# A decoder layer in fp32 on one core: feature blocks of one size, and six gate pieces released by the first slot matrix

## The chip, the cores and the metric

The kernel runs on 1 core of one Trainium2 chip. The metric is device time in microseconds of the whole program, the median of several runs. All tensors are fp32.

## The reference

One layer on a sequence of 256 tokens of width 2048: a conditioning product gives six vectors (shift, scale and gate for two sub-layers); the first sub-layer is one input projection, sparse attention and a pooling branch, and an output projection; the second is a mixture of 32 experts, of which each token uses two.

```
ada = silu(c) @ w_ada + b_ada
sh1, sc1, gt1, sh2, sc2, gt2 = split(ada, 6)
h = rmsnorm(x, g1) * (1 + sc1) + sh1
q, k, v, qi, ki, wi, p = split(h @ w_in)
mix = concat(dsa_attention(...), multiscale_pool(p)) @ w_out
x = x + gt1 * mix
h2 = rmsnorm(x, g2) * (1 + sc2) + sh2
x = x + gt2 * hier_moe(h2)        # top group, top 2 of its 8 experts, SwiGLU
```

`w_ada` has 2048 x 12288 values (100.7 MB), `w_in` 30.5 MB, `w_out` 16.8 MB, and the expert matrices `w1`, `w3`, `w2` 402.7 MB; all are read once.

## The kernel before

**Conditioning, first two vectors.** `sh1` and `sc1` are needed before the input projection can begin. They are made in blocks of features (`BLOCKS`, L184): two blocks of 256 and three of 512. `block_ada(b)` (L188) loads the columns of `w_ada` that a block needs, in pieces of 1 MB, each by two transfers (L201). For the first two blocks TensorE multiplies the pieces with `silu(c)` into PSUM (L209) and ScalarE evicts the sum (L212); for the others VectorE accumulates them (L217, L219). `block_scales(b)` (L223) sums over the partitions by TensorE (L229) and writes scale and shift (L232 to L234).

**Input projection.** The loop at L539 goes over the blocks: scale and shift of the block, `h` of its features (L543), then the seven `PARTS` of `w_in` with these features as the contraction (`project`, L458). Two of the parts accumulate over all blocks in PSUM (L485); the other results are copied at the first block and added by VectorE at the others (`keep`, L466, L470). `w_in` tiles rotate through four slots (`W_RING`: two halves each of `G2` and `G3`). The pieces of the block after this one are issued between the parts. At the last block the indexer and the pooling sums (L516) run as well.

**The other gates.** `fill_steps` (L320) makes `gt1`, `sc2`, `sh2` and `gt2` in 64 pieces of 1 MB of `w_ada` (16 for each vector) and 4 end steps; `fill(n)` (L337) puts the next n steps at the place at which it is called. A piece is one transfer on SP (L177) and one accumulation by VectorE (L178) into half of `G6`. Its slot comes from a ring of three: `G4` at 0, `G4` at 2048, and `G5`; after the attention the third is `B8` (`LATE_RING`, L113). `FILLS` (L538) names the steps at the parts of the last two blocks, L648 and L699 those during the output projection, and L958 what is left before the experts.

**Output projection, router.** `out_proj` (L602) multiplies the pooling half, then the attention half, with `w_out`, in four parts of 512 columns; VectorE multiplies by the gate and adds (L617, L618). In the attention half `route_block(n)` (L674) follows each part: transposes (L679), copies (L681, L682), router products (L686), squares and `x1c` copies. `route_bias` (L666) multiplies `sh2` with the router's weights (L670) and is called after part 2. Behind it comes the router's chain of small VectorE instructions (L708 to L747), five matmul pairs that count ranks (L741 to L745), and `gather(0)` (L781): the slot matrix `gq` (L786), the combine weights (`weights`, L753), the gather by TensorE (L796) and its eviction to `xg` (L800).

**Experts.** For each quad of four experts `hidden` (L808) loads eight tiles of 2 MB in two halves of the contraction: four of `w1`, four of `w3`, for each half (L815). The tiles go through a ring of seven slots, `G5 G1 G2 G3 G0 G7 G4` (L772), to which `G6` is added after the first quad. So the first half takes `G5 G1 G2 G3` for `w1` and `G0 G7 G4 G5` for `w3`. `down` (L850) loads `w2` in the same way.

**What sets the order.** The program is written in dependency order, and the framework's scheduler (L1000) orders each engine's instructions ahead of the run. An engine executes its instructions in that order, and so does SP with its transfers: a transfer that waits for its slot holds up those behind it.

The lines that the change and the steps below touch: L174 to L180, L184, L195 to L213, L538, L700, L740 to L747, L766 to L768, L787 to L789.

Of the kernel before, what the change touches and what calls it, by code (L numbers as in the profile page):

```python
# [11 lines left out]
AF = mybir.ActivationFunctionType  # L12
ALU = mybir.AluOpType
# [66 lines left out]
def layer_kernel(ctx: ExitStack, tc: tile.TileContext, x, c, w_ada, b_ada, norm1_g, w_in, q_norm_g,  # L80
# [92 lines left out]

    def ada_pieces(sec, acc):  # L174
        def piece(k):
            w = slot([P, D], *fill_ring)
            nc.sync.dma_start(w, w_ada[k * P:(k + 1) * P, sec * D:(sec + 1) * D])  # L177
            nc.vector.scalar_tensor_tensor(acc, w, sT[:, k:k + 1], acc, op0=ALU.mult, op1=ALU.add)  # L178

        return [lambda k=k: piece(k) for k in range(KC)]  # L180
# [3 lines left out]
    BLOCKS = [(0, 2), (2, 2), (4, 4), (8, 4), (12, 4)]  # L184
# [3 lines left out]
    def block_ada(b):  # L188


        k0, nk = BLOCKS[b]
        width = nk * P
        acc = bacc[:, b % 2, :, 0:width]
        per = 1024 // width
        ring = (EARLY_RING, "early") if b < 2 else (BLOCK_RING, "block")  # L195
        held = {}

        def piece(q):
            w = slot([P, per, 2, width], *ring)
            for sec in range(2):  # L200
                nc.sync.dma_start(w[:, :, sec], w_ada2[:, q * per:(q + 1) * per, sec, k0 * P:k0 * P + width])  # L201
            if b < 2:
                if q == 0:
                    held["p"] = bank([P, 2, width], "fl")
                pa = held["p"]
                for kk in range(per):
                    k = q * per + kk
                    g = k % 4
                    nc.tensor.matmul(pa[32 * g:32 * (g + 1)], lhsT=sT[:, k:k + 1].to_broadcast([P, 32]), rhs=w[:, kk],  # L209
                                     start=(k < 4), stop=(k >= KC - 4), skip_group_check=True, tile_position=(0, 32 * g))  # L210
                if q == KC // per - 1:
                    nc.scalar.activation(acc, pa, AF.Copy, scale=1.0 / 32.0)  # L212
                return  # L213
            for kk in range(per):
                k = q * per + kk
                if k == 0:
                    nc.vector.tensor_scalar(acc, w[:, kk], sT[:, 0:1], None, op0=ALU.mult)  # L217
                else:
                    nc.vector.scalar_tensor_tensor(acc, w[:, kk], sT[:, k:k + 1], acc, op0=ALU.mult, op1=ALU.add)  # L219

        return [lambda q=q: piece(q) for q in range(KC // per)]
# [316 lines left out]
    FILLS = {3: (0, 0, 0, 0, 1, 1, 1), 4: (4, 4, 4, 3, 3, 3, 3)}  # L538
# [135 lines left out]
    def route_block(n):  # L674
# [25 lines left out]
        if n == 2:  # L700
            route_bias()
# [38 lines left out]
    pr = bank([P, 3, NE], "sm")  # L740
# [3 lines left out]
    nc.tensor.matmul(pr[:, 2], lhsT=ones, rhs=memf[:, 0], start=True, stop=False)  # L744
    nc.tensor.matmul(pr[:, 2], lhsT=ones, rhs=memf[:, 1], start=False, stop=True)  # L745
    pos = small("pos", NE)
    nc.vector.scalar_tensor_tensor(pos, pr[:, 0:2], 1.0, memf, op0=ALU.add, op1=ALU.mult)  # L747
# [5 lines left out]
    def weights():  # L753
# [12 lines left out]
        nc.vector.scalar_tensor_tensor(over, pr[:, 0:2], float(CAP), cmb, op0=ALU.is_ge, op1=ALU.mult)  # L766
        nc.vector.reduce_max(most, pr[:, 2], axis=AX)
# [13 lines left out]
    def gather(e0):  # L781
# [223 lines left out]
```

## Time and profile before

| | us |
|---|---|
| runs: median (lowest to highest of 3) | 1395.92 (1395.58 to 1398.74) |
| profiled execution: time | 1393.28 |
| profiled execution: span of the instructions | 1391.5 |
| busy: TensorE / VectorE / ScalarE / GpSimd | 1071.9 / 447.1 / 100.0 / 9.1 |
| moved by DMA | 557.27 MB, mean 400 GB/s |

A profile is of one execution. Its span runs from the first to the last instruction; the time of the same execution holds 1.8 us more. Busy time says how long an engine had an instruction at work; whether this work sets the end is read from what waits for it. A row `L613 PE MATMUL mm<-g,mix ... x14` is a group of 14 instructions of line 613 on TensorE that read `g` and `mix` and write `mm`; a matmul of the program appears as two instructions. In brackets stands how long the engine had been idle before it, and what ended that. `PE` is TensorE, `PEld` its weight loads, `DVE` VectorE, `ACT` ScalarE, `POOL` GpSimd, `SP` the engine that issues most transfers.

### The profile page before, as it was taken

To read this page: it belongs to the slowest core of one execution; us is meant where nothing else is said; L and a number is where in the kernel's file an instruction comes from. 1 tells how busy PE (TensorE), PEld (TensorE's weight loads), DVE (VectorE), ACT (ScalarE), POOL (GpSimd) and SP (SyncE) were. 2 spreads that over 40 slices of the span, in tenths; PEclk is the share of its full clock that TensorE was granted. 3 is DMA by queue.
4 is the path that set the end of the run, shared out by engine and by line. 5 is a ranking of instruction groups with operands and counts; after the bars stand their busy time and mean duration, and the time that the engine had idled before them with its cause. 6 is when DMAs were issued, how large, how long until landed. Compare 5 with 4: busy or idle time off the path is not lost.

```text
span 1391.5 us, 12491 instructions
## 1 busy us (share of the span) xinstructions
PE 1071.9 (77%) x5227; PEld 433.6 (31%) x5227; DVE 447.1 (32%) x725; ACT 100.0 (7%) x225; POOL 9.1 (1%) x11
## 2 busy tenths in 40 slices
PE   4899998998997776677758767676776766777566
PEld 2455654544456231122213113121321311222112
DVE  1196667999677210201202111020220202012002
ACT  3200000424222000000000000000000000000000
POOL 1000000000000000000000000000000000000000
PEclk9999999999997979879979988997998998898789
DMA  9999998999999799999999999999999999999997
GB/s 320 328 385 385 400 386 324 342 361 322 400 365 405 325 427 428 427 428 427 427 429 428 428 429 426 427 428 428 428 429 427 428 427 427 428 429 428 429 424 283
DMA packets 101259, 557.27 MB, mean 400 GB/s; under 512 B 18792, under 2 KB 31056, under 8 KB 68688
## 3 DMA queue, kind: packets, MB, share of 16 engines
q1 hardware_dynamic: 97664, 554.22, 97.9%
q10 hardware_dynamic: 3472, 2.20, 0.5%
q8 instruction: 43, 0.70, 0.2%
q14 instruction: 16, 0.13, 0.0%
q0 software_dynamic: 64, 0.02, 0.0%
HBM read 554.31 MB, written 2.10 MB: 400 GB/s over the span
## 4 chain that ended last, share of the span: by engine, by line
DMA 52%; PE 33%; DVE 9%; issue 3%; SPq 2%; ACT 1%; ACTq 0%; DVEq 0%
DMA w<-in_w_dram 49%; PE mm L820 11%; PE mm L475 5%; PE mm L613 5%; PE b L861 4%; PE b L485 3%; DVE g L178 3%; DMA g<-in_w_in_dram 2%; DMA g<-in_w_ada_dram 1%; PE b L877 1%; DVE bacc L219 1%; SPq L815 1%; PE b L796 1%; DVE g L408 1%; DMA v8T<-in_b_ada_dram 1%
## 5 line engine op out<-in xcount | busy, mean ns | idle before, releaser
L820 PE MATMUL mm<-w,xg 128*32 128x512 f32 x2048 | 341.9, 704 | 162.8 <-DMA w<-in_w_dram 162.8
L861 PE MATMUL b<-w,t 128*32 128x512 f32 x896 | 178.0, 671 | 86.5 <-DMA w<-in_w_dram 81.0
L820 PEld LDWEIGHTS mm<-w,xg 128*32 128x32 f32 x2048 | 76.9, 126 | 415.1 <-DMA w<-in_w_dram 229.0
L800 DVE TENSOR_SCALAR xg<-b,sc2T,sh2T 128x128 f32<-128x128 f32 x128 | 42.3, 404 | 390.8 <-PE b L796 390.8
L475 PE MATMUL mm<-g,hT 128*128 128x512 f32 (+1 forms) x320 | 127.6, 553 | 12.0 <-DMA g<-in_w_in_dram 7.1
L178 DVE SCALAR_TENSOR_TENSOR g<-g,sT,g 128x2048 f32<-128x2048 f32 x52 | 122.0, 2346 | 12.2 <-DMA g<-in_w_ada_dram 12.1
L613 PE MATMUL mm<-g,mix 128*128 128x512 f32 x256 | 114.8, 601 | 4.2 <-DVE t L617 4.2
L861 PEld LDWEIGHTS b<-w,t 128*32 128x32 f32 x896 | 41.9, 116 | 217.6 <-DMA w<-in_w_dram 120.5
L841 DVE TENSOR_TENSOR t<-b,gt 128x512 f32<-128x512 f32 (+1 forms) x33 | 20.9, 671 | 273.0 <-PE b L861 250.7
L475 PEld LDWEIGHTS mm<-g,hT 128*128 128x128 f32 x320 | 57.2, 199 | 78.3 <-issue 64.2
L613 PEld LDWEIGHTS mm<-g,mix 128*128 128x128 f32 x256 | 48.2, 193 | 60.7 <-issue 55.1
L844 PE MATMUL mm<-t,gwT 128*128 128x512 f32 (+1 forms) x132 | 62.6, 605 | 3.3 <-DVE t L841 2.8
L796 PEld LDWEIGHTS b<-gq,x1c 128*128 128x128 f32 x512 | 59.8, 196 | 13.1 <-issue 6.7
L796 PE MATMUL b<-gq,x1c 128*128 128x128 f32 x512 | 62.7, 282 | 1.2 <-DVE gq L786 1.2
L824 ACT ACTIVATE t<-mm 128x512 f32<-128x512 f32 x8 | 4.8, 597 | 816.7 <-PE mm L820 816.7
L485 PE MATMUL b<-hT,g 128*128 128x256 f32 x256 | 56.9, 380 | 0.5 <-DMA g<-in_w_in_dram 0.4
L485 PEld LDWEIGHTS b<-hT,g 128*128 128x128 f32 x256 | 48.4, 190 | 11.2 <-issue 3.2
L846 DVE TENSOR_TENSOR xs<-xs,mm 128x512 f32<-128x512 f32 (+1 forms) x66 | 44.3, 671 | 17.7 <-PE mm L844 17.5
L825 DVE TENSOR_TENSOR t<-t,mm 128x512 f32<-128x512 f32 x8 | 5.5, 688 | 116.3 <-PE mm L820 116.3
L219 DVE SCALAR_TENSOR_TENSOR bacc<-g,sT,bacc 128x1024 f32<-128x1024 f32 x28 | 35.9, 1283 | 7.1 <-DMA g<-in_w_ada_dram 4.6
L844 PEld LDWEIGHTS mm<-t,gwT 128*128 128x128 f32 x132 | 21.2, 188 | 45.2 <-DVE xs L846 28.4
L178 DVE SCALAR_TENSOR_TENSOR g<-w,sT,g 128x2048 f32<-128x2048 f32 x12 | 28.1, 2346 | 2.3 <-DMA w<-in_w_ada_dram 2.2
(208 smaller groups left out, 514.4 us busy)
## 6 DMA issues: line engine op xcount, KB each, us to landing
w<-in_w_dram SPq DMA_DIRECT2D x190, 2048.0 KB, 21.3
g<-in_w_ada_dram SPq DMA_DIRECT2D x52, 1024.0 KB, 8.3
g<-in_w_ada_dram SPq DMA_DIRECT2D x44, 512.0 KB, 9.5
g<-in_w_in_dram SPq DMA_DIRECT2D x21, 1024.0 KB, 10.9
g<-in_w_out_dram SPq DMA_DIRECT2D x16, 1024.0 KB, 9.5
w<-in_w_ada_dram SPq DMA_DIRECT2D x12, 1024.0 KB, 7.4
w<-in_w_ada_dram SPq DMA_DIRECT2D x20, 512.0 KB, 9.7
g<-in_w_in_dram SPq DMA_DIRECT2D x14, 512.0 KB, 8.7
```

Of the source, the lines that this page charges most:

```text
L178: nc.vector.scalar_tensor_tensor(acc, w, sT[:, k:k + 1], acc, op0=ALU.mult, op1=ALU.add)
L219: nc.vector.scalar_tensor_tensor(acc, w[:, kk], sT[:, k:k + 1], acc, op0=ALU.mult, op1=ALU.add)
L475: nc.tensor.matmul(po[:, :width], lhsT=hcols(k0 + j, slice(i * P, (i + 1) * P)), rhs=w[:, j], start=(j == 0), stop=(j == nk - 1))
L485: nc.tensor.matmul(ppool[n][:, u], lhsT=w[:, j, u * P:(u + 1) * P], rhs=hcols(k, slice(0, S)), start=(k == 0 and u % 2 == 0), stop=(k == K ...
L613: nc.tensor.matmul(po, lhsT=mix[:, k, i * P:(i + 1) * P], rhs=ws[k // 4][:, k % 4], start=(k == 0), stop=(k == 7))
L796: nc.tensor.matmul(px[:, u], lhsT=x1c[i][:, k // RB, k % RB], rhs=gq[:, i].rearrange("p e s -> p (e s)"), start=(i == 0), stop=(i == NT - 1))
L800: nc.vector.tensor_scalar(xg[:, k], px[:, u], sc2T[:, k:k + 1], sh2T[:, k:k + 1], op0=ALU.mult, op1=ALU.add)
L820: nc.tensor.matmul(h[e * CAP:(e + 1) * CAP, :], lhsT=xg[:, k, e * CAP:(e + 1) * CAP], rhs=ws[e][:, r], start=(k == 0), stop=(k == KC - 1), ...
L841: nc.vector.tensor_mul(y[:, 0:m], py, gt2[:, c0:c0 + m])
L844: nc.tensor.matmul(pz[:, 0:m], lhsT=gwT[:, i], rhs=y[:, 0:m], start=True, stop=True)
L846: nc.vector.tensor_add(xv, xv, pz[:, 0:m])
L861: nc.tensor.matmul(py[n // 2][e * CAP:(e + 1) * CAP, (n % 2) * 512:(n % 2 + 1) * 512], lhsT=aT[:, f, e * CAP:(e + 1) * CAP], rhs=ws[e][:, ...
```

## The change

The first two parts belong to the front of the program. `BLOCKS` has four blocks of 512 features. Only the first is multiplied by TensorE, into two banks instead of one, and its pieces hold 2 rows of 512 values per section where they held 4 of 256; its `w_in` tiles hold four contraction rows instead of two. `FILLS` names the same steps at the last two blocks.

`route_bias` is called one part earlier. The rank counts keep three of five matmul pairs; the two for the maximum go into a bank of their own, inside `weights()`. `weights()` and the product of the combine weights move behind the gather. `gather(0)` puts one column of its slot matrix into `behind`; a piece of `w_ada` that is emitted after that first gets this column copied into its slot by VectorE, and its transfer is issued on GpSimd's queue instead of SP's. These are the last six pieces of `gt2`. The copy is overwritten by the transfer.

```diff
+    behind = []
+
     def ada_pieces(sec, acc):
         def piece(k):
             w = slot([P, D], *fill_ring)
-            nc.sync.dma_start(w, w_ada[k * P:(k + 1) * P, sec * D:(sec + 1) * D])
+            if not behind:
+                nc.sync.dma_start(w, w_ada[k * P:(k + 1) * P, sec * D:(sec + 1) * D])
+            else:
+                nc.vector.tensor_copy(w[:, 0:1], behind[0])
+                nc.gpsimd.dma_start(w, w_ada[k * P:(k + 1) * P, sec * D:(sec + 1) * D])
             nc.vector.scalar_tensor_tensor(acc, w, sT[:, k:k + 1], acc, op0=ALU.mult, op1=ALU.add)
...
-    BLOCKS = [(0, 2), (2, 2), (4, 4), (8, 4), (12, 4)]
+    BLOCKS = [(0, 4), (4, 4), (8, 4), (12, 4)]
...
-        ring = (EARLY_RING, "early") if b < 2 else (BLOCK_RING, "block")
+        ring = (EARLY_RING, "early") if b == 0 else (BLOCK_RING, "block")
...
-                    held["p"] = bank([P, 2, width], "fl")
-                pa = held["p"]
+                    held["p"] = [bank([P, width], "mm") for _ in range(2)]
...
-    FILLS = {3: (0, 0, 0, 0, 1, 1, 1), 4: (4, 4, 4, 3, 3, 3, 3)}
+    FILLS = {2: (0, 0, 0, 0, 1, 1, 1), 3: (4, 4, 4, 3, 3, 3, 3)}
...
-        if n == 2:
+        if n == 1:
             route_bias()
...
-    nc.tensor.matmul(pr[:, 2], lhsT=ones, rhs=memf[:, 0], start=True, stop=False)
-    nc.tensor.matmul(pr[:, 2], lhsT=ones, rhs=memf[:, 1], start=False, stop=True)
...
-        nc.vector.reduce_max(most, pr[:, 2], axis=AX)
+        pm = bank([P, NE], "fl")
+        nc.tensor.matmul(pm, lhsT=ones, rhs=memf[:, 0], start=True, stop=False)
+        nc.tensor.matmul(pm, lhsT=ones, rhs=memf[:, 1], start=False, stop=True)
+        nc.vector.reduce_max(most, pm, axis=AX)
...
         if e0 == 0:
-            weights()
-        nc.vector.tensor_mul(gw, gw, bc(cmb[:, :, e0:e0 + QE, None], QE, CAP))
+            behind.append(gq[:, 1, 0, 0:1])
...
+        if e0 == 0:
+            weights()
+        nc.vector.tensor_mul(gw, gw, bc(cmb[:, :, e0:e0 + QE, None], QE, CAP))
```

**Where instructions move: SP at the start.** Here `g_70`, `g_71`, `g_72` are `G4`, `G5`, `G6`, and `g_68`, `g_69` the slots of `w_in`. Before, behind the transfer of `x`:

```order
L148 DMA xs<-in_x_dram 128x2048 x2
L201 DMA g_70<-in_w_ada_dram 128x4x256 x4
L201 DMA g_71<-in_w_ada_dram 128x4x256 x2
L201 DMA g_72<-in_w_ada_dram 128x4x256 x4
L463 DMA g_68<-in_w_in_dram 128x2x512
L201 DMA w<-in_w_ada_dram 128x4x256 x2
L463 DMA g_68<-in_w_in_dram 128x2x512
L463 DMA g_69<-in_w_in_dram 128x2x512 x2
L625 DMA wr<-in_w_exp_dram 128x8x32
L201 DMA g_70<-in_w_ada_dram 128x4x256 x2
```
After:

```order
L148 DMA xs<-in_x_dram 128x2048 x2
L208 DMA g_70<-in_w_ada_dram 128x2x512 x4
L208 DMA g_71<-in_w_ada_dram 128x2x512 x2
L208 DMA g_72<-in_w_ada_dram 128x2x512 x4
L208 DMA w<-in_w_ada_dram 128x2x512 x2
L471 DMA g_68<-in_w_in_dram 128x4x512 x2
L208 DMA g_70<-in_w_ada_dram 128x2x512
L471 DMA g_69<-in_w_in_dram 128x4x512 x2
L633 DMA wr<-in_w_exp_dram 128x8x32
L208 DMA g_70<-in_w_ada_dram 128x2x512 x3
```
Before, the first eight transfers of `w_ada` are the first block, and the `w_in` tiles come behind them. Now the first block is 16 transfers: the twelve ahead of the first `w_in` tile, and four among the tiles and the router's weights.

**VectorE at the first slot matrix.** Before, from the slots' comparison on (`w` and `g4` are the slots of the pieces, `g6` the accumulator of `gt2`):

```order
L784 TENSOR_TENSOR t2_1899<-kc_76,pos_1892 128x256
L768 CAST mosti_1897<-most_1896 128x1
L786 TENSOR_SCALAR gq_1898<-t2_1899,rs2_1857 128x128 x2
L789 TENSOR_TENSOR t2_1899<-t2_1899,cmb_1894 128x256
L178 SCALAR_TENSOR_TENSOR g6_72<-w_1983,sT_102,g6_72 128x2048
L178 SCALAR_TENSOR_TENSOR g6_72<-g4_70,sT_102,g6_72 128x2048
L800 TENSOR_SCALAR xg_1920<-b2_1921,sc2T_1478,sh2T_1651 128x128 x8
L800 TENSOR_SCALAR xg_1920<-b2_1946,sc2T_1478,sh2T_1651 128x128 x8
L805 COPY gwT_1974<-sm_1971 128x256
L178 SCALAR_TENSOR_TENSOR g6_72<-g4_70,sT_102,g6_72 128x2048
```
After, from the second line behind the slot matrix on (the maximum, L776, stands between):

```order
L811 TENSOR_TENSOR t2_1863<-t2_1863,cmb_1858 128x256
L183 COPY w_1943<-gq_1862 128x1
L777 CAST mosti_1861<-most_1860 128x1
L183 COPY g4_70<-gq_1862 128x1 x2
L808 TENSOR_SCALAR xg_1867<-b2_1868,sc2T_1444,sh2T_1617 128x128 x8
L808 TENSOR_SCALAR xg_1867<-b2_1893,sc2T_1444,sh2T_1617 128x128 x8
L816 COPY gwT_1941<-sm_1938 128x256
L185 SCALAR_TENSOR_TENSOR g6_72<-w_1943,sT_102,g6_72 128x2048
L185 SCALAR_TENSOR_TENSOR g6_72<-g4_70,sT_102,g6_72 128x2048
L183 COPY w_1953<-gq_1862 128x1
L185 SCALAR_TENSOR_TENSOR g6_72<-g4_70,sT_102,g6_72 128x2048
L183 COPY g4_70<-gq_1862 128x1 x2
```
Two of the last three accumulations stood ahead of the evictions to `xg`; now all six stand behind them, and the copies that release the second three pieces stand among these accumulations.

**SP at the first expert loads.** With each tile's number: before, `w_2034`, `w_2036`, `w_2038` are the second to fourth tile of `w3` of the first half (in `G7`, `G4`, `G5`), `w_2072` to `w_2078` those of `w1` of the second half:

```order
L815 DMA w_2034<-in_w3_dram 128x4096
L177 DMA g4_70<-in_w_ada_dram 128x2048
L971 TENSOR_LOAD mosti_1897
L971 ISA x2
L815 DMA w_2036<-in_w3_dram 128x4096
L815 DMA w_2038<-in_w3_dram 128x4096
L815 DMA w_2072<-in_w1_dram 128x4096
L815 DMA w_2074<-in_w1_dram 128x4096
L815 DMA w_2076<-in_w1_dram 128x4096
L856 DMA w_2285<-in_w2_dram 128x4096
```
After, `w_2007`, `w_2009`, `w_2011` are the same three of `w3` (in `G7`, `G4`, `G5`), and `w_2045` to `w_2051` those of `w1`:

```order
L826 DMA w_2007<-in_w3_dram 128x4096
L982 TENSOR_LOAD mosti_1861
L982 ISA x2
L826 DMA w_2011<-in_w3_dram 128x4096
L826 DMA w_2045<-in_w1_dram 128x4096
L826 DMA w_2047<-in_w1_dram 128x4096
L826 DMA w_2049<-in_w1_dram 128x4096
L826 DMA w_2009<-in_w3_dram 128x4096
L826 DMA w_2051<-in_w1_dram 128x4096
L826 DMA w_2085<-in_w3_dram 128x4096
L826 DMA w_2087<-in_w3_dram 128x4096
```
The tile in `G4` stood ahead of the three for the second half; now it stands behind them and behind the tile in `G5`. TensorE uses the four tiles of a half in turn for each contraction row.

## Rows read from the trace of the kernel before

**Rows 1.** The page's slices of 34.8 us each: mean rate of transfers.
```profile
GB/s 320 328 385 385 400 386 324 342 361 322 400 365 405 325 427 428 427 428 427 427 429 428 428 429 426 427 428 428 428 429 427 428 427 427 428 429 428 429 424 283
```

**Rows 2.** Windows: us; busy PE, PEld, DVE, ACT, POOL; PE clock; DMA share; GB/s.
```profile
0.00:12.50 12.50, 0.00 (x0) 0.00 (x0) 0.39 (x2) 0.76 (x1) 0.20 (x4) 1.00 0.86 279
...
12.50:25.00 12.50, 7.50 (x32) 3.53 (x33) 3.59 (x9) 6.19 (x9) 0.00 (x0) 1.00 1.12 337
...
56.00:130.00 74.00, 69.83 (x256) 41.89 (x256) 54.39 (x60) 8.12 (x16) 0.00 (x0) 0.98 1.05 385
...
220.00:240.00 20.00, 16.39 (x55) 7.44 (x54) 20.00 (x34) 0.17 (x1) 0.00 (x0) 0.91 0.89 323
...
320.00:340.00 20.00, 13.36 (x55) 7.93 (x54) 19.89 (x30) 7.44 (x27) 2.29 (x2) 0.91 0.91 315
...
336.00:422.50 86.50, 85.27 (x260) 42.46 (x261) 67.71 (x59) 27.25 (x59) 0.00 (x0) 0.98 0.95 353
...
445.50:460.00 14.50, 14.44 (x118) 10.66 (x122) 13.35 (x24) 0.00 (x0) 0.00 (x0) 0.89 0.52 216
...
460.00:465.00 5.00, 4.33 (x27) 1.14 (x16) 1.01 (x4) 0.59 (x1) 0.00 (x0) 1.00 0.88 308
```

**Rows 3.** TensorE in order of time, to 345 us: start, duration, engine, line, operation.
```profile
30.42 1.05 PE L229 MATMUL sm<-ones,bacc 128*128 128x1 f32 x8 [0.72 <-ACT bacc L212]
...
32.55 3.72 PE L485 MATMUL b<-hT,g 128*128 128x256 f32 x16
...
56.07 13.18 PE L475 MATMUL mm<-g,hT 128*128 128x80 f32 x32 [4.68 <-DMA g<-in_w_in_dram]
...
97.53 7.07 PE L485 MATMUL b<-hT,g 128*128 128x256 f32 x32
...
202.30 13.98 PE L485 MATMUL b<-hT,g 128*128 128x256 f32 x64
```

**Rows 4.** Groups of VectorE's instructions, 216 to 345 us: busy, mean ns | idle before.
```profile
L178 DVE SCALAR_TENSOR_TENSOR g<-g,sT,g 128x2048 f32<-128x2048 f32 x23 | 54.0, 2346 | 0.0
...
L575 DVE SCALAR_TENSOR_TENSOR g<-b,g 128x1024 f32<-128x1024 f32 x2 | 2.4, 1219 | 0.0
...
L578 DVE TENSOR_REDUCE mx<-g 128x4 f32<-128x1024 f32 x2 | 2.4, 1197 | 0.0
```

**Rows 5.** TensorE in order of time, 395 to 500 us.
```profile
411.13 1.42 PE L686 MATMUL sm<-ws,g 128*128 128x36 f32 x12
...
432.64 3.60 PE L686 MATMUL sm<-ws,g 128*128 128x36 f32 x16 [0.39 <-DVE brt L672]
...
443.31 0.61 PE L744 MATMUL sm<-mem,ones 128*128 128x32 f32 x2
...
445.56 8.94 PE L796 MATMUL b<-gq,x1c 128*128 128x128 f32 x64 [1.20 <-DVE gq L786]
...
454.64 7.94 PE L820 MATMUL mm<-w,xg 128*32 128x512 f32 x68
...
472.65 8.76 PE L820 MATMUL mm<-w,xg 128*32 128x512 f32 x60 [2.63 <-DMA w<-in_w_dram]
```

**Rows 6.** VectorE in order of time, 395 to 480 us.
```profile
423.19 2.34 DVE L178 SCALAR_TENSOR_TENSOR g<-w,sT,g 128x2048 f32<-128x2048 f32 x1
...
428.46 0.69 DVE L682 COPY g<-b 128x512 f32<-128x512 f32 x1 [1.11 <-ACT g L681]
...
438.66 2.33 DVE L178 SCALAR_TENSOR_TENSOR g<-g,sT,g 128x2048 f32<-128x2048 f32 x1
...
457.42 2.35 DVE L178 SCALAR_TENSOR_TENSOR g<-g,sT,g 128x2048 f32<-128x2048 f32 x1
```

**Rows 7.** DMA issues: count, KB each, median us to landing.
```profile
g<-in_b_ada_dram POOLq DMA_DIRECT2D x2, 8.0 KB, 5.4
```

**Rows 8.** SP's issues in order of time, 458 to 486 us.
```profile
459.79 4.89 SPq L815 DMA_DIRECT2D w<-in_w_dram  x5
...
480.58 1.75 SPq L815 DMA_DIRECT2D w<-in_w_dram  x4
```

More of the change, by code (lines that the diff above doesn't have):

```diff
@@ L201, in piece @@
                 nc.sync.dma_start(w[:, :, sec], w_ada2[:, q * per:(q + 1) * per, sec, k0 * P:k0 * P + width])
-            if b < 2:
+            if b == 0:
                 if q == 0:
-                    held["p"] = bank([P, 2, width], "fl")
-                pa = held["p"]
+                    held["p"] = [bank([P, width], "mm") for _ in range(2)]
                 for kk in range(per):
@@ L208, in piece @@
                     g = k % 4
-                    nc.tensor.matmul(pa[32 * g:32 * (g + 1)], lhsT=sT[:, k:k + 1].to_broadcast([P, 32]), rhs=w[:, kk],
-                                     start=(k < 4), stop=(k >= KC - 4), skip_group_check=True, tile_position=(0, 32 * g))
+                    for sec, pa in enumerate(held["p"]):
+                        nc.tensor.matmul(pa[32 * g:32 * (g + 1)], lhsT=sT[:, k:k + 1].to_broadcast([P, 32]), rhs=w[:, kk, sec],
+                                         start=(k < 4), stop=(k >= KC - 4), skip_group_check=True, tile_position=(0, 32 * g))
                 if q == KC // per - 1:
-                    nc.scalar.activation(acc, pa, AF.Copy, scale=1.0 / 32.0)
+                    for sec, pa in enumerate(held["p"]):
+                        nc.scalar.activation(acc[:, sec], pa, AF.Copy, scale=1.0 / 32.0)
                 return
@@ L737, in layer_kernel @@
     nc.vector.tensor_scalar(memf, lz, THRESH, None, op0=ALU.is_lt)
-    pr = bank([P, 3, NE], "sm")
+    pr = bank([P, NT, NE], "sm")
     nc.tensor.matmul(pr[:, 0], lhsT=tri, rhs=memf[:, 0], start=True, stop=True)
@@ L743, in layer_kernel @@
     nc.tensor.matmul(pr[:, 1], lhsT=tri, rhs=memf[:, 1], start=False, stop=True)
-    nc.tensor.matmul(pr[:, 2], lhsT=ones, rhs=memf[:, 0], start=True, stop=False)
-    nc.tensor.matmul(pr[:, 2], lhsT=ones, rhs=memf[:, 1], start=False, stop=True)
     pos = small("pos", NE)
-    nc.vector.scalar_tensor_tensor(pos, pr[:, 0:2], 1.0, memf, op0=ALU.add, op1=ALU.mult)
+    nc.vector.scalar_tensor_tensor(pos, pr, 1.0, memf, op0=ALU.add, op1=ALU.mult)
     cmb, over = small("cmb", NE), small("over", NE)
@@ L765, in weights @@
         nc.vector.tensor_mul(cmb, cmb, bc(sg, NE))
-        nc.vector.scalar_tensor_tensor(over, pr[:, 0:2], float(CAP), cmb, op0=ALU.is_ge, op1=ALU.mult)
-        nc.vector.reduce_max(most, pr[:, 2], axis=AX)
+        nc.vector.scalar_tensor_tensor(over, pr, float(CAP), cmb, op0=ALU.is_ge, op1=ALU.mult)
+        pm = bank([P, NE], "fl")
+        nc.tensor.matmul(pm, lhsT=ones, rhs=memf[:, 0], start=True, stop=False)
+        nc.tensor.matmul(pm, lhsT=ones, rhs=memf[:, 1], start=False, stop=True)
+        nc.vector.reduce_max(most, pm, axis=AX)
         nc.vector.tensor_copy(mosti, most)
```

## The prediction

> **What bounds the kernel now.** The page's slices come first: from about 490 us on, the kernel moves 424 to 429 GB/s in every slice but the last, so that part is bound by transfers; before it the rate is between 320 and 405 [rows 1]. The number of bytes does not change. So the end moves by what happens to the moment at which the expert loads begin to run without a break, by what is still unloaded then, and by any break after it.
>
> The windows show what holds the front [rows 2]. Over 0 to 12.5 us 279 GB/s arrive, at 12.5 to 25 us, with `w_ada` in rows of 256 values, 337, and from 56 to 130 us, with rows of 512 values throughout, 385 at a full queue. From 220 to 240 and 320 to 340 us VectorE is busy for 20.00 and 19.89 of 20 us while TensorE stands for 3.6 and 6.6 us: VectorE is the bound there. From 336 to 422.5 us TensorE is busy for 85.27 of 86.5 us: the output projections bound that stretch. From 445.5 to 460 us only 216 GB/s are moved, because no slot is free. TensorE's order in time [rows 3] shows the projections start at 32.55 us, wait 4.68 us until 56.07, and then go on, with the third block (the first of 512 features) at 97.53 and the last block at 202.30 us.
>
> **The first block.** The changed kernel loads 16 half-megabyte transfers of `w_ada` for its first block, where the old one needed 8, and two pairs of `w_in` stand among them in SP's order. Up to the last of the 16, SP has issued `x` 2.1 MB, constants 0.2, `w_ada` 8.4, four `w_in` 4.2 and one router transfer 0.1, or 15.0 MB. By 12.5 us 279 GB/s make 3.5 MB; the other 11.5 MB at 385 GB/s take 29.9 us, so 42.4 us, and I add 1 us for the router transfer's short rows. The matmuls of the last half and the step to the projections follow: the old kernel needed 2.85 us from its last accumulation (the eviction that ends at 30.42 follows one that began at 29.70) to 32.55; eight more column sums take 1.05 us [rows 3]. That gives a start at about 48 us instead of 32.55. The old third and fourth blocks took (202.30 - 97.53) / 2 = 52.4 us each with their waits; the new first block has the same size, so the second starts at 100.4 us, where the old kernel had the same state at 97.53: **+2.9 us**. The early start of the old kernel is worth little because it pays the wait until 56.07 and eight products for the second block in between. Loading 8.4 MB in the longer rows saves 24.9 - 21.8 = 3.1 us of transfers, but the projections, not the transfers, pace the blocks; it is covered, and already in the 385 used above. The block fewer of partial sums (11 additions) falls where VectorE has free time, and costs and gains nothing while the projections go on.
>
> **The middle.** Between the pooling sums and the product of the last pool projection, VectorE's order now holds 26 accumulations of gate pieces where it held 28 (one was moved ahead, one behind), and the last head group's logits and their maximum come after it. At 2.346, 1.219 and 1.197 us [rows 4] this is 4.7 + 2.4 = **-7.1 us**. The work is not gone: it lies beside TensorE's full stretch, where VectorE has 18.8 us free. Bounds of this and the first term together: +5.9 (nothing saved here, and `w_in` comes 3 us late at the second block) and -7.3 us (all 10.2 us of TensorE's idle time in the two windows vanish). I take the sum, -4.2.
>
> **From the output projection to the slot matrices.** `route_bias` moves into TensorE's full stretch. It has 32 instructions; in the full stretch, instructions of the same shape take 1.42 / 12 = 0.118 us [rows 5], so **+3.8 us** (bounds 0, if a hole takes it, and 7.2, at the pace of the 16 at 432.64). In the chain behind, these disappear: the accumulation of 2.34 us between the product and the sum of the last part; the wait for `brt` from the ready copy (428.46 + 0.69) to 432.64, 3.5 us; the accumulation of 2.33 us at 438.66 [rows 6]; two of five matmul pairs of the ranks, from 443.31 on, 0.9 us [rows 5]. Together **-9.0 us**. With `weights()` behind the gather, only `over` stays ahead of the slot matrix, so 0.2 us more is left out.
>
> **The six pieces.** The slot matrix releases them, through one-column copies. Three slots exist, so three pieces can go at once, on POOL's queue. Nothing deep ran on that queue before: an 8 KB transfer took 5.4 us to land on it [rows 7]. At 428 GB/s three pieces (3.15 MB) take 7.35 us, so from the slot matrix (I call the start of its gather g, the old 445.56) they land by about g + 14, in the old gap. Their accumulations stand behind both groups of evictions in VectorE's order, at g + 12 to g + 19, and only they free the slots for the other three. Now the resumption: the first 64 expert instructions ended at 454.64 + 7.5 = 462.1, g + 16.5 [rows 5]; the old SP went on at 459.79, g + 14.2, when the last accumulation at 457.42 [rows 6] freed `G4`, and issued five expert loads [rows 8]. The new SP goes on at g + 16.5, **+2.3 us**, and the three other pieces (3.15 MB) are still to be loaded: **+7.35 us**, as they share the running transfers.
>
> **The slot G4.** Both halves of `G4` hold late pieces, so the third load of the first `w3` half, which needs `G4`, now stands behind four later loads, and SP issues it when the last piece is accumulated, near g + 38. All transfers in flight then end with it: 8.4 + 3.15 + 2.1 MB from g + 18, about g + 50. Every other ring slot is full or in use, and TensorE needs this tile before it can free one. It works through 60 instructions, which took from 472.65 [rows 5] to SP's next issue at 480.58 [rows 8], 7.9 us; the old kernel had further loads queued beside that. Add the landing's signal and the next start: the 308 GB/s of 460 to 465 us [rows 2] are 3.6 us of flow, so the first bytes came at 461.4, 1.6 us after the issue; two loads (4.2 MB) from there should be in at 471.2, and TensorE began at 472.65, 1.4 us later. A new break of **+10.9 us** (bounds 7.9 without these signals, and 16 if POOL's pieces come last).
>
> **Sum.** +2.9 - 7.1 + 3.8 - 9.0 + 2.3 + 7.35 + 10.9 = +11.15 us, about +11. The profiled execution took 1393.28 us around a span of 1391.5, and goes to 1404.4; the median of the runs stands 2.6 us above it, so 1407.
>
> A rule beside the late pieces: on the Trainium skill's page "DMA: Bandwidth & Descriptors" (Queues, rings and completion order) each DMA engine takes turns between the queues that have work, packet by packet. By that rule the three late pieces would not wait for SP's four loads, and the time would be that of the sum and not that of the second rival. No row here shows two deep queues at once.
>
> **The rivals.** (1) My forecast, slower by about 11 us: chance 0.60.
> (2) POOL's pieces are served behind SP's four loads. These 8.4 MB end at g + 38, the pieces at g + 45.6, and the accumulations and the issue of `G4` come some 5 us after the last transfer: +16 us, 1412. For it: the 5.4 us of the only POOL row. Decided by the landing time of the last three pieces. 0.16.
> (3) All six pieces fit into the gap, since the releases come faster than I read them; then the 7.35 us go and +3.8 us is left, 1400, no change that can be told (about 0.3%, 4.2 us, is what a measurement of this kernel tells from none). Against it: the accumulations' place in VectorE's order. 0.12.
> (4) Faster: the output projections are paced by transfers, not by TensorE. Then six pieces less shorten 336 to 422.5 us by 6.3 MB / 428 GB/s = 14.7 us and hide `route_bias`: 11.15 - 14.7 - 3.8 = -7.4, 1388.6. For it: the DMA share of 0.95 in that window [rows 2]. Against it: TensorE idles only 1.2 us there. It decides from the point where a projection waits for `w_out` at all. 0.12. The Trainium skill's page "Trainium Kernel Development and Optimization" (Performance Expectations) calls matmul busy time a bad metric, since matmuls are pipelined. By that rule 85.27 us of busy time would not exclude this rival; the rows at hand agree so far as their instructions of one shape differ in time by the place at which they stand (0.118 and 0.225 us).
>
> **The numbers.** The likeliest gives 1407. Low end: the first terms at -7.3 (3.1 lower) and the break at 7.9 (3.0 lower), one late piece in the gap (2.45): 1398. High end: the second rival, with the first terms near their upper bound: 1417. Slower is 0.60 + 0.16 = 0.76, the same 0.12, faster 0.12.
>
> **What would show it.** Projections that start near 48 us; the second block near 100; no accumulation of gate pieces between the last output projection and the slot matrix, and some 14 us between these two; six `w_ada` transfers on POOL's queue, the first three in the gap, the others beside expert loads; then a slice some 30 us later in which the rate falls, with TensorE at 60 expert instructions and SP waiting for it. The prediction is wrong if no such break is there, if the steady rate begins earlier than before with all of `w_ada` loaded, or if the output projections end much earlier than 422 us.

## The result, and the profile after

The changed kernel takes 1415.16 us in the median of 4 runs (1413.23 to 1417.21), the kernel before 1395.75 beside it: a ratio of 1.0134, 95% interval 1.0118 to 1.0150, so 1.2 to 1.5% slower. Forecast were 1407 and a range of 1398 to 1417. The profiled execution took 1415.19 us around a span of 1413.4, 21.9 more than the span before. The sign and the places were right; the forecast size was little more than half of what came.

The page's slices, as [rows 1] of before:

```profile
GB/s 347 288 382 384 400 376 324 356 384 316 366 316 327 366 291 428 428 428 427 428 427 428 427 429 426 429 426 428 428 428 425 429 429 427 426 429 428 428 425 283
```
The slice from 494.7 to 530.0 us (the fifteenth) has 291 GB/s, between slices of 366 and 428: the new break is there. From then on the rate is what it was.

TensorE in order of time in the front, as [rows 3]:

```profile
42.80 4.92 PE L216 MATMUL mm<-g,sT 128*32 128x512 f32 x12 [5.74 <-DMA g<-in_w_ada_dram]
48.43 1.95 PE L237 MATMUL sm<-ones,bacc 128*128 128x1 f32 x16 [0.70 <-ACT bacc L220]
51.46 5.12 PE L493 MATMUL b<-hT,g 128*128 128x256 f32 x16 [1.08 <-ACT hT L551]
...
99.28 2.83 PE L493 MATMUL b<-hT,g 128*128 128x256 f32 x12
101.95 3.60 PE L483 MATMUL mm<-g,hT 128*128 128x512 f32 x8
...
207.59 13.98 PE L493 MATMUL b<-hT,g 128*128 128x256 f32 x64
...
336.65 13.04 PE L621 MATMUL mm<-g,mix 128*128 128x512 f32 x30
```
and of the kernel before, at the output projection:

```profile
336.43 9.10 PE L613 MATMUL mm<-g,mix 128*128 128x512 f32 x17 [3.45 <-DVE t L617]
```
The input projections start at 51.46 us (forecast 48). At 99.28 the second block has begun, but eight matmul instructions of the first (3.60 us) still stand behind it, so it is really at 102.9, where the old kernel was at 97.53. The last block starts at 207.59 instead of 202.30, 5.3 us late. The first output projection behind VectorE's full stretch starts at 336.65, where the old one started at 336.43 (its wait of 3.45 us ended there): there the changed kernel is only 0.2 us late.

VectorE from the first pooling sum to the first product of the last pool projection, of the kernel before:

```profile
217.36 2.28 DVE L516 TENSOR_TENSOR wa<-g 128x2040 f32<-128x2040 f32 x1 [9.52 <-ACT g L488]
...
348.24 0.68 DVE L617 TENSOR_TENSOR t<-mm,gt 128x512 f32<-128x512 f32 x1
```
and of the changed kernel:

```profile
222.65 2.28 DVE L524 TENSOR_TENSOR wa<-g 128x2040 f32<-128x2040 f32 x1 [9.52 <-ACT g L496]
...
346.13 0.68 DVE L625 TENSOR_TENSOR t<-mm,gt 128x512 f32<-128x512 f32 x1
```
130.9 us have become 123.5. The accumulations of gate pieces in this stretch are 26 where they were 28, and one logits instruction of 1.22 us and one maximum of 1.20 us of the last head group now come behind it.

TensorE from the router's bias on, as [rows 5]:

```profile
418.18 3.66 PE L678 MATMUL sm<-wr,sh2T 128*128 128x36 f32 x32
...
421.85 7.03 PE L621 MATMUL mm<-g,mix 128*128 128x512 f32 x16
...
439.88 0.61 PE L749 MATMUL sm<-mem,kc 128*128 128x32 f32 x2 [3.68 <-DVE mem L745]
...
442.44 9.51 PE L804 MATMUL b<-gq,x1c 128*128 128x128 f32 x64 [0.25 <-DVE gq L795]
...
452.10 7.92 PE L831 MATMUL mm<-w,xg 128*32 128x512 f32 x68
475.42 1.89 PE L831 MATMUL mm<-w,xg 128*32 128x512 f32 x2 [15.41 <-DMA w<-in_w_dram]
482.75 1.91 PE L831 MATMUL mm<-w,xg 128*32 128x512 f32 x2 [5.45 <-DMA w<-in_w_dram]
489.07 1.92 PE L831 MATMUL mm<-w,xg 128*32 128x512 f32 x2 [4.40 <-DMA w<-in_w_dram]
490.92 2.08 PE L298 MATMUL fl<-g,ones 128*128 128x512 f32 x2
...
496.41 2.07 PE L298 MATMUL fl<-g,ones 128*128 128x512 f32 x2 [0.67 <-ACT gt L299]
498.42 8.56 PE L831 MATMUL mm<-w,xg 128*32 128x512 f32 x60
```
and the last output projection of the kernel before:

```profile
416.37 6.17 PE L613 MATMUL mm<-g,mix 128*128 128x512 f32 x14
```
The last output projection ends at 421.85 + 7.03 = 428.88 us, 6.3 after the old one, and the gather starts at 442.44, 13.6 us behind it, where the old kernel needed 23.0. Behind the first 68 instructions (64 of them of `w1`) TensorE stands for 15.4 us, then does one matmul at a time as loads land, then three column sums of `gt2` (L298), and only at 498.42 the 60 instructions of `w3` that free the slots.

VectorE at the last three pieces, as [rows 6]:

```profile
461.91 0.27 DVE L183 COPY g<-gq 128x1 f32<-128x1 f32 x2
472.64 2.35 DVE L185 SCALAR_TENSOR_TENSOR g<-w,sT,g 128x2048 f32<-128x2048 f32 x1 [10.46 <-DMA w<-in_w_ada_dram]
480.09 2.35 DVE L185 SCALAR_TENSOR_TENSOR g<-g,sT,g 128x2048 f32<-128x2048 f32 x1 [5.09 <-DMA g<-in_w_ada_dram]
487.46 2.35 DVE L185 SCALAR_TENSOR_TENSOR g<-g,sT,g 128x2048 f32<-128x2048 f32 x1 [5.02 <-DMA g<-in_w_ada_dram]
```
Two of them were released at 461.91 (the first at 459.53), and they land one in 7.4 us. GpSimd's issues of late pieces have a median of 10.4 and 14.9 us to landing, where the 8 KB of [rows 7] had 5.4.

Windows of 2.5 us (columns as in [rows 2]):

```profile
455.00:457.50 2.50, 2.50 (x28) 0.78 (x24) 2.46 (x2) 0.00 (x0) 0.00 (x0) 1.00 0.03 13
...
460.00:462.50 2.50, 0.01 (x2) 0.00 (x0) 2.18 (x3) 0.00 (x0) 0.64 (x2) 1.00 0.98 295
...
485.00:487.50 2.50, 0.00 (x0) 0.00 (x0) 0.04 (x1) 0.00 (x0) 0.00 (x0) 0.50 1.01 429
487.50:490.00 2.50, 0.93 (x2) 0.18 (x2) 2.50 (x2) 0.00 (x0) 0.00 (x0) 0.50 0.10 39
490.00:492.50 2.50, 2.50 (x4) 0.50 (x2) 1.06 (x4) 0.00 (x0) 0.00 (x0) 0.50 0.69 184
...
495.00:497.50 2.50, 1.83 (x3) 0.50 (x2) 0.00 (x0) 0.59 (x1) 0.00 (x0) 0.50 0.54 229
497.50:500.00 2.50, 2.50 (x10) 0.40 (x12) 0.00 (x0) 0.59 (x1) 0.00 (x0) 0.50 0.04 7
...
505.00:507.50 2.50, 2.50 (x18) 0.64 (x10) 0.00 (x0) 0.00 (x0) 0.00 (x0) 1.00 0.32 66
507.50:510.00 2.50, 0.54 (x2) 0.00 (x0) 0.00 (x0) 0.59 (x1) 0.00 (x0) 1.00 0.81 315
```
The loads go on at 460.8 us and stop at 487.7, 2.1 MB (the tile in `G4`) pass from 491.4 to 496.3, and the flow begins again at 507.8 (counted at 428 GB/s; the first bytes come near 507, at a lower rate). TensorE's clock stands at 0.50, the lower of its levels (1.2 of 2.4 GHz), from 487.5 to 500 us; it had been idle from 460.0 to 475.4.

**One account for every run.** Take the moment at which the expert loads begin to run without a break (the start of the 5 us window plus what it misses to 428 GB/s), the 7.35 us of late pieces still to come at that moment, and the later breaks (what the windows miss to 428 GB/s, summed). What is left of the span is the same in all kernels:

| kernel | loads run from | pieces | breaks | rest | span |
|---|---|---|---|---|---|
| before | 461.4 | 0 | 0 | 930.1 | 1391.5 |
| before, second profile | 466.7 | 0 | 0 | 930.4 | 1397.1 |
| changed | 460.8 | 7.35 | 15.1 | 930.2 | 1413.4 |
| blocks alone | 466.1 | 0 | 0 | 930.5 | 1396.6 |
| no late pieces | 466.8 | 0 | 0 | 931.2 | 1398.0 |
| three late pieces | 461.1 | 0 | 6.4 | 930.3 | 1397.8 |
| two queues | 461.0 | 7.35 | 15.6 | 929.7 | 1413.6 |
| six pieces, `w3` in pairs | 462.3 | 7.35 | 14.4 | 930.2 | 1414.2 |
| two queues, no sums | 461.3 | 7.35 | 6.2 | 930.5 | 1405.4 |
| three pieces, `w3` in pairs | 464.0 | 0 | 0.6 | 930.6 | 1395.2 |
| the same, five blocks | 462.1 | 0 | 0 | 929.9 | 1392.0 |
| router's edits alone | 462.7 | 0 | 0 | 930.2 | 1392.9 |

The pieces and the breaks are 22.45 us; against them the loads resume 0.6 us earlier than in the first profile of before, where the terms of the forecast gave 7.1. The medians lie 19.4 apart and the profiles 21.9, since the first profile of before is 2.5 us below the median beside it. Against the second profile of before the loads resume 5.9 us earlier.

### The profile page after: what moved, and what is told of

The parts are those of the page before. It is cut to its first block, busy times and chain, and to the rows that moved or that the text cites. A ratio compares the mean times of both kernels' runs of the same rounds, so it can differ in the third digit from the quotient of the medians.

```text
span 1413.4 us, 12461 instructions
## 1 busy us (share of the span) xinstructions
PE 1078.0 (76%) x5227; PEld 433.0 (31%) x5227; DVE 443.1 (31%) x717; ACT 99.4 (7%) x225; POOL 12.3 (1%) x17
## 4 chain that ended last, share of the span: by engine, by line
DMA 56%; PE 32%; DVE 6%; SPq 2%; issue 2%; ACT 1%; ACTq 0%; DVEq 0%
DMA w<-in_w_dram 49%; PE mm L831 10%; PE mm L483 5%; DMA g<-in_w_ada_dram 4%; PE b L872 4%; PE mm L621 3%; PE b L493 3%; DVE g L185 2%; DMA g<-in_w_in_dram 2%; PE b L888 1%; SPq L826 1%; DVE g L416 1%; DMA v8T<-in_b_ada_dram 1%; PE fl L298 1%; PE b L804 1%
## 5 line engine op out<-in xcount | busy, mean ns | idle before, releaser
L872 PE MATMUL b<-w,t 128*32 128x512 f32 x896 | 183.2, 690 | 82.8 <-DMA w<-in_w_dram 77.4
L483 PE MATMUL mm<-g,hT 128*128 128x512 f32 (+1 forms) x320 | 123.6, 539 | 3.5 <-DMA g<-in_w_in_dram 1.9
## 6 DMA issues: line engine op xcount, KB each, us to landing
g<-in_w_ada_dram POOLq DMA_DIRECT2D x4, 1024.0 KB, 14.9
```

The lines of the kernel that those rows point to most:

```text
L483: nc.tensor.matmul(po[:, :width], lhsT=hcols(k0 + j, slice(i * P, (i + 1) * P)), rhs=w[:, j], start=(j == 0), stop=(j == nk - 1))
L872: nc.tensor.matmul(py[n // 2][e * CAP:(e + 1) * CAP, (n % 2) * 512:(n % 2 + 1) * 512], lhsT=aT[:, f, e * CAP:(e + 1) * CAP], rhs=ws[e][:, ...
```

## The experiments

Each edit is against the changed kernel where nothing else is said.

**The blocks alone** (the kernel before with the four blocks).

```diff
-    BLOCKS = [(0, 2), (2, 2), (4, 4), (8, 4), (12, 4)]
+    BLOCKS = [(0, 4), (4, 4), (8, 4), (12, 4)]
...
-    FILLS = {3: (0, 0, 0, 0, 1, 1, 1), 4: (4, 4, 4, 3, 3, 3, 3)}
+    FILLS = {2: (0, 0, 0, 0, 1, 1, 1), 3: (4, 4, 4, 3, 3, 3, 3)}
```

> The kernel before with the four blocks of 512 alone. Theory A (the late pieces and the tile in G4 make the loss, the blocks a small part): in the changed kernel the last block began 5.3 us late (207.59 instead of 202.30) and some 2 us of that came back at VectorE's waits, so 3 us slower, 1397 to 1400. Theory B (the blocks make the loss, since the front keeps TensorE waiting longer and all that follows moves with it): 10 us or more, 1406 or later. Theory C (the expert part is paced by transfers, and what the front loses is taken back at the gap of the slots): no change, 1394 to 1397.

1398.36 us (1394.96 to 1400.56), ratio 1.0014 (1.0002 to 1.0027): some 2 us, as theory A has it. TensorE in order of time:

```profile
207.87 13.98 PE L486 MATMUL b<-hT,g 128*128 128x256 f32 x64
...
449.32 9.60 PE L797 MATMUL b<-gq,x1c 128*128 128x128 f32 x64 [1.20 <-DVE gq L787]
```
The last block is as late as in the changed kernel, so that delay belongs to the blocks. So does what comes back of it: the first output projection behind VectorE's full stretch starts at 336.93 us here.

**No late pieces.**

```diff
-        if e0 == 0:
-            behind.append(gq[:, 1, 0, 0:1])
```

> The changed kernel without the late pieces: nothing is put into the list that holds them back, so all of w_ada goes through SP as before; the blocks, the router's bias one part earlier and the weights behind the gather stay. Theory A: the 7.35 us of the three pieces still to be loaded and the break at G4 (15.1 us by the sum of what the windows from 487.5 to 512.5 us miss to 428 GB/s) go, and some of it is given back by accumulations that return to VectorE ahead of the slot matrix: 1392 to 1398, no change to slightly faster than before. Theory B: it keeps most of the loss, 1405 or later.

1398.20 us (1396.04 to 1399.72), ratio 1.0009 (0.9999 to 1.0019), 0.2 us above what theory A gave. No break is left: from 470 to 700 us every window of 5 us has 419 GB/s or more. The late pieces make the loss.

**Three late pieces.**

```diff
         if n < 2:
             fill(9)
+        if n == 2:
+            fill(3)
```

> The changed kernel with three late pieces instead of six: three more steps of the gate pieces are emitted at part 2 of the output projection, so that only one round of the three slots is released by the slot matrix. Theory A: the first three land in the gap (they were accumulated by 462 us in the changed kernel), so neither the 7.35 us nor the break of 15.1 us is left: 1415 - 22 = 1393, within 3 us. A rival: the break comes from the place of the tile in G4 behind four other loads on SP, which is the same here, whether or not a second round is there: then only the 7.35 us go, 1408.

1402.69 us (1399.94 to 1404.88), ratio 1.0052 (1.0033 to 1.0070): between the two. The 7.35 us are gone, and so is more than half of the break, but not all. TensorE, and the windows:

```profile
482.08 1.91 PE L833 MATMUL mm<-w,xg 128*32 128x512 f32 x2 [2.98 <-DMA w<-in_w_dram]
486.98 8.95 PE L833 MATMUL mm<-w,xg 128*32 128x512 f32 x60 [2.98 <-DMA w<-in_w_dram]
```
```profile
490.00:492.50 2.50, 2.50 (x24) 0.68 (x20) 0.00 (x0) 0.00 (x0) 0.00 (x0) 0.84 0.18 66
...
495.00:497.50 2.50, 0.92 (x8) 0.01 (x2) 0.00 (x0) 0.00 (x0) 0.00 (x0) 1.00 0.61 144
```
The pieces are long in, and still TensorE waits for the tile in `G4` until 486.98, since four loads stand ahead of it on SP. Its 60 instructions then take 8.95 us; one load (of `w2`, into `G6`) covers the first 3.4 us of that, and 6.4 us are lost before the flow is full again.

**Two queues for the late pieces.**

```diff
-                nc.gpsimd.dma_start(w, w_ada[k * P:(k + 1) * P, sec * D:(sec + 1) * D])
+                (nc.gpsimd if k % 2 == 0 else nc.scalar).dma_start(w, w_ada[k * P:(k + 1) * P, sec * D:(sec + 1) * D])
```

> The changed kernel with every second late piece on ScalarE's queue instead of GpSimd's. In the changed kernel the last three pieces landed at 472.6, 480.1 and 487.4 us, one in 7.4 us, in which 3.15 MB flow: one piece of 1.05 MB (rows of 8 KB) for each expert load of 2.1 MB (rows of 16 KB). Theory A (queues take turns row by row): with two queues beside SP's two pieces share half of the flow and land in 9.8 us, the third in 7.35 more, so the last at 478 instead of 487.4; G4 is issued at 481, its transfer follows the others without a break, and TensorE goes on at about 493.5 instead of 498.4: 4 to 6 us less than the changed kernel, 1409 to 1411. A rival (pieces end with SP's loads whatever their queue, because the engines serve what was issued first): no change, 1415.

1414.59 us (1411.37 to 1415.58), ratio 1.0122: no gain. VectorE's last accumulation and TensorE:

```profile
481.96 2.35 DVE L185 SCALAR_TENSOR_TENSOR g<-g,sT,g 128x2048 f32<-128x2048 f32 x1 [2.78 <-DMA g<-in_w_ada_dram]
```
```profile
489.26 1.92 PE L831 MATMUL mm<-w,xg 128*32 128x512 f32 x2 [2.98 <-DMA w<-in_w_dram]
...
498.60 8.86 PE L831 MATMUL mm<-w,xg 128*32 128x512 f32 x60
```
The queues do share: the last piece is in 5.5 us earlier (9 were expected), and the flow goes on until 492.7. But TensorE takes up the 60 instructions at 498.60, as before, behind the sums. So neither the pieces nor `G4` were the last wait of the break, and the theory of this run falls; that the sums were the last wait is tested below.

**`w3` in pairs**, so that `G0` and `G7` come free without the tile in `G4`.

```diff
-                for r in range(RB):
-                    k = kb * RB + r
-                    for e in range(QE):
+                first = e0 == 0 and kb == 0 and wx is w3
+                for pair in ((0, 1), (2, 3)) if first else (range(QE),):
+                    for r in range(RB):
+                        k = kb * RB + r
+                        for e in pair:
```

> The changed kernel, with the matmuls of the first half of w3 in another order: first the experts in G0 and G7 through all contraction rows, then the two in G4 and G5, so that G0 and G7 come free without the tile in G4. Theory A (the break is TensorE holding every slot until G4 has landed): G0 and G7 are refilled while the last pieces are on their way, and the break of 15.1 us shrinks to 0 to 4 us: 1400 to 1404. A rival (the break is made by what stands behind the last piece: its accumulation, the sums of gt2 on TensorE and the half clock, and shifts with them): at most the 4.9 us of the transfer of G4 are hidden, 1409 to 1413.

1416.11 us (1413.45 to 1418.56), ratio 1.0148: the expectation failed, and for a reason that it did not have. TensorE, and windows of 2.5 us:

```profile
453.50 13.93 PE L833 MATMUL mm<-w,xg 128*32 128x512 f32 x96
...
537.66 1.92 PE L833 MATMUL mm<-w,xg 128*32 128x512 f32 x2 [15.87 <-DMA w<-in_w_dram]
542.53 9.33 PE L833 MATMUL mm<-w,xg 128*32 128x512 f32 x60 [2.96 <-DMA w<-in_w_dram]
```
```profile
540.00:542.50 2.50, 0.00 (x0) 0.00 (x0) 0.00 (x0) 0.00 (x0) 0.00 (x0) 0.50 0.17 72
...
550.00:552.50 2.50, 1.86 (x16) 0.33 (x8) 0.49 (x1) 0.00 (x0) 0.00 (x0) 1.00 0.50 92
```
After 96 instead of 68 instructions two slots are free, the flow no longer stops at 487.7, and only 2.1 us are lost near 505. But a break of 12.3 us stands at 540 to 552: with other slots free at other times the scheduler put two tiles of the second half of `w3` behind four of `w2`, and there the same thing happens. All slots are full, and the 60 instructions that free them wait for the tiles issued last.

**The pairs with three late pieces**: the two edits above together.

> Three late pieces instead of six and the same order of the matmuls. With three pieces the break was 6.4 us (the windows from 490 to 500 us) and nothing was left to load. Theory A: the break goes, 1402.7 - 6.4 = 1396. The rival: as with three pieces alone, 1402.

1395.70 us (1394.10 to 1398.33), ratio 0.9998 (0.9986 to 1.0009). Here the break goes and does not come back: theory A.

**The same with five blocks**: also `BLOCKS`, `FILLS` and the first block's matmuls as in the kernel before.

> As the last, with the five blocks of the kernel before. The four blocks alone brought the slot matrix 3.8 us later (449.32 instead of 445.56). If this carries over, 1396 - 3.8 = 1392, 3 to 4 us faster than the kernel before. A rival (the gap before the expert loads takes up what the front gains): 1395 to 1396.

1395.01 us (1393.05 to 1397.57), ratio 0.9994 (0.9984 to 1.0004): the rival. Its gather starts at 443.18 us, but the loads resume at 462.1, behind the first 64 expert instructions, and not earlier than in the first profile of the kernel before.

**The router's edits alone**: five blocks as there, `fill(9)` as in the changed kernel, `w3` not in pairs, and no late pieces (the lines with `behind.append` left out).

> The kernel before with the router's bias one part earlier and the weights behind the gather alone (five blocks, no late pieces). With four blocks these two moved the time by nothing (1398.2 beside 1398.4), since the accumulations ahead of the slot matrix take what the shorter chain gives: if so, 1394 to 1397. A rival (the chain of 0.9 + 3.5 us is gained): 1391 to 1393.

1397.57 us (1394.74 to 1398.33), ratio 1.0003 (0.9991 to 1.0015): nothing, as expected, with the median 0.6 us above the expected range. TensorE:

```profile
441.55 0.61 PE L748 MATMUL sm<-mem,kc 128*128 128x32 f32 x2 [9.18 <-DVE mem L744]
```
It waits 9.18 us for the mask there, since VectorE has three accumulations of gate pieces ahead of it (431.40, 434.25 and 436.98 us); 5.97 in the kernel without late pieces, 3.68 in the changed one.

**Two queues, and no sums of `gt2`.**

```diff
-            pt = bank([P, 512], "fl")
-            nc.tensor.matmul(pt, lhsT=ones, rhs=acc[:, n * 512:(n + 1) * 512], start=True, stop=True)
+            pt = acc[:, n * 512:(n + 1) * 512]
+            if name == "gt1":
+                pt = bank([P, 512], "fl")
+                nc.tensor.matmul(pt, lhsT=ones, rhs=acc[:, n * 512:(n + 1) * 512], start=True, stop=True)
             nc.scalar.copy(gt[:, n * 512:(n + 1) * 512], pt)
```

> The changed kernel with two queues for the late pieces, and without the sums of gt2 over the partitions: ScalarE copies the accumulator itself, so the four matmuls with ones for gt2 are left out, and the gate is not the reference's. With two queues the pieces landed 5.5 us earlier (the last one at 481.9 instead of 487.4 us) and the tile in G4 followed without a break until 492.7, but TensorE began its 60 instructions at 498.6, no earlier than before, because three of the sums stood ahead of them, each waiting for ScalarE's copy of the one before at half clock (491.1 to 498.6). Theory A (these sums are the part of the break that I had not priced): TensorE begins near 493, G6 comes free earlier and takes a tile of w2 in the meantime, and the break shrinks from 15.6 to 5 or 6 us: 1403 to 1407. A rival (the break is set by the 60 instructions and the signals around them, and the sums hide behind the landing of G4): 1411 to 1415.

1408.69 us (1405.95 to 1411.35), ratio 1.0084 (1.0057 to 1.0110), 5.9 less than with two queues alone (8.2 in the profiles); the median is 2 us above the range of theory A, the break with 6.2 us nearly where it had it. The kernel leaves the sums out, so its gate is not the reference's. TensorE:

```profile
494.63 9.04 PE L833 MATMUL mm<-w,xg 128*32 128x512 f32 x60 [3.01 <-DMA w<-in_w_dram]
```
The 60 instructions begin 4.0 us earlier, and `G6`, free without the sums, takes one more load (4.9 us) meanwhile. What this run does not tell apart is how much of the 9.4 us by which the break shrinks each of the two gives.

**A second profile of the kernel before**, without an edit.

> The kernel before once more, for a second profile of it: the first one took 1393.28 us, 2.6 below the median. From the first moment of unbroken expert loads to the end it took 930.2 us, and the other kernels the same within 0.6 us (their breaks and late pieces taken off). If the scatter of a kernel's runs lies ahead of that moment, this profile shows the same 930 us, and its moment differs from 461.3 by what its span differs from 1391.5.

1398.84 us, span 1397.1. TensorE at the gather, and the window at the resumption:

```profile
450.45 9.37 PE L796 MATMUL b<-gq,x1c 128*128 128x128 f32 x64 [1.20 <-DVE gq L786]
```
```profile
465.00:467.50 2.50, 2.50 (x24) 0.70 (x19) 1.34 (x5) 0.00 (x0) 0.00 (x0) 1.00 0.61 157
```
The gather starts 4.9 us later than in the first profile, the loads 5.3 (466.7), and the rest is 930.4 us. So the scatter between these two lies ahead of the expert loads, and it grows on the way: 0.4 us at the last block (202.71), 1.9 at the first output projection behind VectorE's full stretch (338.30), 3.7 at the end of the projections. A difference of 4 or 5 us at the gather between single profiles, such as the 3.8 us of the blocks alone, is therefore not shown to belong to an edit. By the account and the median of before (1396) its loads usually resume near 464; the changed kernel's gather stood at 441.8 to 443.9 in the four profiles that share its front.

## Why the prediction was right in sign and too small

**The first block: +2.9 forecast, +5.3 measured.** The transfers came when forecast: the last 12 matmul instructions of the block begin at 42.80 us. What failed is the tail behind them: 2.85 + 1.05 us were taken, and it was 8.7 (42.80 to 51.46), since the 12 matmul instructions alone take 4.92 and the eviction, 16 instructions of column sums and `h` follow. The length of the block (52.4 forecast, 51.5 measured from 51.46 to 102.9) was right.

**The middle: -7.1 forecast, -2.7 kept.** On VectorE the term was right, in its parts and its size: 7.4 us less in that stretch. TensorE's gain at the first output projection behind it was 5.1 (from 5.3 late to 0.2). The step that failed is the one that took this as a gain in full, up to the slot matrix. To the end of the projections 2.4 us of it go again (6.3 late there, of which 3.7 are the bias): work of the last head groups on TensorE, which had stood inside the waits, now stands behind them. From 336 us to the end of the projections the changed kernel has 8 matmul instructions of L580 (1.9 us), 2 more of L605 (1.1) and 4 more of L601 (0.4); the old one had none of the same line (its L572) and fewer of the others. These are single profiles, but all twelve agree: the last block begins at 201.29 to 202.71 us in the four with five blocks and at 206.45 to 207.87 in the eight with four; the first output projection behind VectorE's full stretch at 336.3 to 338.3 and 335.3 to 338.7; and from there to the end of the projections, the bias taken off where it stands among them, they take 86.0 to 87.9 and 88.3 to 89.0 us.

**Router.** The bias took 3.66 us (3.8 forecast), the chain 13.6 instead of 23.0, -9.5 (-9.0 forecast). That they are worth nothing by themselves shows in the run with the router's edits alone: where pieces are still accumulated ahead of the slot matrix, the chain waits for those. There the gather starts 18.1 us behind the projections, 4.9 less than in the kernel before, and the bias, now among the projections, takes 3.7 of that.

**Resumption: +2.3 forecast, +2.5 measured** (18.35 instead of 15.84 us behind the gather). **Three pieces left: +7.35**, as the account shows.

**The break: +10.9 forecast, 15.1 measured.** Its mechanism was right: TensorE holds every slot until the tile in `G4` is in and its 60 instructions are done, and the run with three pieces and pairs, in which two slots come free without that tile, has no break. Two steps were mis-sized. The forecast had the last piece accumulated near g + 38 and `G4` issued with other loads still in flight; it was accumulated at 489.8, g + 47.4, when nothing was in flight, so the break has a first part of 3.7 us (487.7 to 491.4). The second part, 496.3 to 507.8, is 11.4 us, near the 10.9 forecast, but not made of what was forecast: 8.56 us of instructions (7.9 read), 2.1 us until the sums were done, which the forecast had not priced, and 0.8 to the full flow. The clock may have a part in the 2.1 us: at 0.50 the sums follow each other in 2.75 us, at 1.00 in the kernel with the blocks alone in 1.80; at that pace, as an estimate, the third would have been done by 495.6, before `G4` had landed. No run tests this.

**How the pieces shared the queues.** From the first landing on, 1.05 MB of a piece pass beside 2.1 MB of an expert load in 7.4 us (3.15 MB at 428 GB/s), and the matmuls at 475.42, 482.75 and 489.07 show those loads landing each 1.5 to 3 us behind a piece. The rows of a piece hold 8 KB, those of an expert load 16. By the Trainium skill, "DMA: Bandwidth & Descriptors" (Queues, rings and completion order), an engine takes turns between queues packet by packet. The trace agrees: while the second of these pieces landed, from 472.7 to 480.1 us, the queue of the loads (q1) and that of the pieces (q0) moved nearly the same number of packets (packets, MB, share of the 16 engines' time):

```profile
q1 hardware_dynamic: 145, 2.11, 66.7%
q0 software_dynamic: 146, 1.07, 34.0%
```
In the run with two queues the three queues moved 120, 116 and 117 packets from 466 to 474 us. But the 2.11 MB are 128 rows of 16 KB and the 1.07 MB 128 rows of 8 KB, each with a few small packets, so the turns are not equal shares of the bytes: a third went to the pieces. The first of the three landed at 472.64, since its packets begin only between 464 and 465 us, though it was issued at 459.97. So rival (2), pieces behind SP's loads, was wrong in its mechanism and nearly right in its moment (g + 45.6 forecast, g + 45.0 measured), since a third of the flow ends as late.

Rivals (3) and (4) did not come. The second three pieces were released at 459.53 and 461.91 us, behind accumulations that stand behind the evictions, so the gap from 455 to 460.8 us stayed empty (13 GB/s from 455.0 to 457.5) instead of taking them. The projections with six pieces less ended 6.3 us later, not earlier; from 336.65 us on TensorE stood idle ahead of their matmuls for 1.1 us in all, and what ended that were VectorE's products, never a transfer of `w_out`:

```profile
L621 PE MATMUL mm<-g,mix 128*128 128x512 f32 x160 | 71.0, 594 | 1.1 <-DVE t L625 1.1
```

The sum, by the first profile of before: 5.3 - 2.7 + 3.7 - 9.5 + 2.5 + 7.35 + 15.1 = 21.75, beside 21.9 measured. Of the 10.6 us that the forecast lacked, the middle has 4.4, the break 4.2 and the first block 2.4, and 2.5 us of the 10.6 belong to that profile, which is so much faster than the median. The large errors point the same way, so no luck hides one behind another; that the measured median lies inside the range, 2 us below its upper end, owes something to how wide the range was. Its upper end was also added up short: the second rival's 1412 with the first terms at +5.9 in place of -4.2 gives 1422, not 1417.

## What to carry to other kernels

Where everything behind a point runs at the rate of the transfers, price an edit by three things alone: when the loads begin to run without a break, what is still unloaded then, and each later break. Before a slot of a ring is given to late work, look at which instructions free the other slots: if they need the tile of that slot, the ring runs dry for their whole length plus whatever stands ahead of them on their engine. And when work leaves an engine that others wait for, look at what those did during the waits; a part of it can come back behind them.

## What the runs showed that I had not expected

Two queues with deep work shared packet for packet and not byte for byte: a queue with 8 KB rows beside one with 16 KB rows got a third of the flow (other sizes were not tried). TensorE's granted clock fell to 0.50 in an idle stretch of 15.4 us and stayed there until 500 us, far into the break, so that a pair of instructions took 1.9 us and a column sum 2.07, where the kernel with the blocks alone shows 1.04 and 1.12 at 1.00. And the scatter of the runs, 5.6 us between two profiles of one kernel, lay ahead of the expert loads but for 0.3 us; the 930 us behind them agreed within 1.5 us in twelve profiles.
